# The transpose in a triangular inverse from TensorE in place of a masked merge, beta moved into the decay, and a new plan

## The chip, the cores and the metric

One core of a Trainium2 chip runs the whole program. The metric is device time in microseconds (us) of one execution. An engine is one of five units with an instruction queue of its own that runs in order: TensorE (PE; PEld is its weight load), VectorE (DVE), ScalarE (ACT), GpSimd (POOL) and SyncE (SP, which issues loads).

## The reference, cut to what matters

A two-layer encoder on 256 tokens of width 1024, in float32. Each layer projects the tokens with a wide matrix, runs three mixers side by side (differential attention, a gated delta rule in both directions, windowed attention), merges them through gates, and ends in a gated MLP; each half closes with a layer norm. The change lies in the delta rule, which solves one unit triangular system per head, chunk and direction:

```python
decay = jnp.exp(jnp.where(incl, gc[..., :, None] - gc[..., None, :], -jnp.inf))
kk = jnp.einsum('bhncd,bhnsd->bhncs', kb, k) * decay      # kb = k * beta
a_mat = jnp.where(strict, kk, 0.0) + jnp.eye(C, dtype=kk.dtype)
sol = lax.linalg.triangular_solve(a_mat, rhs, left_side=True, lower=True, unit_diagonal=True)
```

## The kernel before, in words

The weights come in blocks of 512 KB. Each is split on chip into two fp32r parts: ScalarE (or VectorE) copies the block to `hi`, VectorE subtracts to `lo`, and TensorE runs three matmuls for each product (`mm3`). A block thus costs one 128x1024 pass on either engine and, in a channel-major projection, 24 matmuls. There are four `hi`/`lo` pairs (WBUFS) and four landing tiles (RBUFS).

Nothing is issued in the order of the text. Every call on an engine is recorded by `Plan.record` with a cost from `_cost`; `Plan.emit` gives each a rank (the longest chain of costs and of `LATENCY` to the end, plus a priority from `PRIO` by label), and `Plan.schedule` lays the calls out in time, engine by engine. The calls are then issued in the order of these start times, so each engine's queue is fixed beforehand. `A.copy`, `A.scale` and `A.affine` (class `Either`) may go to ScalarE or VectorE, as the plan finds better. The order of the weight blocks is written out (`ORDER`), and their loads keep it (`stream`). All recorded calls carry the line 194 in the profile, so tiles tell them apart.

The delta rule is `gdn`. `decay` makes, for each direction d and half tt of the tokens, exp of the decay differences for four heads (dt_, tag D; 128x512) and a strictly triangular copy (ds_, tag N) by two `affine_select` on GpSimd. Later, `gdn` multiplies k times k (pk, in PSUM), minus beta and ds_ into the matrix N, one head at a time. `solve` then inverts eight 128x128 matrices of one direction at once, by doubling: levels of block size 1, 2, 4, ... 64. It holds the inverse so far (xx) and its transpose (y), both f16. For each level from the second on it makes pv = nt16 x (half of xx), copies it to v16, then makes pp = v16 x (half of y) and px = y x (half of v16); pp is merged into y and px into xx, through a mask with `copy_predicated` for blocks under 32 and by plain copies of sub-blocks above. The two directions run interleaved. pv, pp and px are 8 matmuls each, of 128x64, and each group fills one PSUM bank of the kind "ch", of which there are two (`BANKS`). In the rows, `ch_solve<-a,b` names the moving operand first: `h_solve` is nt16, xx or y, `v_solve` is v16, `id` the identity.

Of the kernel before, what the change touches and what calls it, by code (L numbers as in the profile page):

```python
# [75 lines left out]
def _cost(eng, name, outs, ins, args, kw):  # L76
# [28 lines left out]
    return 0.069 + n / 960 / fast + 0.061 * sum(_columns(ap) == 1 for ap in ins)  # L105
# [32 lines left out]
class Plan:  # L138
# [43 lines left out]
    def record(self, *ways):  # L182
# [36 lines left out]
        op.load = (0.108 if ins[0].dtype in (F32, F32R) else 0.055) if eng == "PE" else 0.0  # L219
# [1283 lines left out]
```

## Time and profile before

| | |
|---|---|
| runs of the kernel | 1000.6 us median of 3 (999.37 to 1002.41) |
| profiled execution | 1000.26 us, of which the span from first to last instruction is 998.6 |
| TensorE clock granted | 0.996 of full speed |
| busy: TensorE / weight load / VectorE / ScalarE / GpSimd | 972.1 / 909.3 / 741.0 / 568.5 / 72.4 us |

How to read it: busy time is the time in which at least one instruction of the engine runs. Idle time of an engine is put down to what released the next instruction. The rows that matter stand two sections below. The stretches with a name in them are: 30 to 50 and 520 to 545 us (`decay` of layer 0 and 1), 70 to 120 and 560 to 612 us (the two solves), 350 to 400 us (a plain stretch of the MLP's projections).

### The profile page before, as it was taken

What the parts mean: (1) busy time and instruction counts of PE and PEld (TensorE: products, weight loads), DVE (VectorE), ACT (ScalarE), POOL (GpSimd) and SP (SyncE); (2) the same over time, 40 slices, a digit from 0 to 9 for tenths busy, and PEclk for the clock granted to TensorE, in tenths of its full rate; (3) what the DMA queues carried; (4) which work ended last, traced back from release to release, by engine and by line L of the source; (5) the groups of instructions that cost most, each with busy time, mean ns of one, the idle gap of its engine ahead of it and who ended that gap; (6) DMA issues with size and microseconds to landing.
All of it is one profiled execution on the core that took longest, in us unless ns stands there. A gap on an engine that the chain in (4) does not pass through costs nothing.

```text
span 998.6 us, 19140 instructions
## 1 busy us (share of the span) xinstructions
PE 972.1 (97%) x7598; PEld 909.3 (91%) x7598; DVE 741.0 (74%) x1362; ACT 568.5 (57%) x1012; POOL 72.4 (7%) x84
## 2 busy tenths in 40 slices
PE   7999999999999999999999989999999999999996
PEld 6898899998988999998889979999999889999885
DVE  7799985675589766675688997866646995677655
ACT  5666865665455654544545876566744655455441
POOL 0510010100000100000006100000000110000000
PEclk9999999999999999999999999999999999999998
DMA  7553344454575655565625423343545855555651
GB/s 269 181 170 100 117 122 151 149 166 140 188 242 167 212 195 188 172 190 188 213 85 190 143 87 119 130 130 111 168 149 174 284 180 164 189 190 177 204 190 43
DMA packets 50109, 165.43 MB, mean 166 GB/s; under 512 B 5751, under 2 KB 11271, under 8 KB 50020
## 3 DMA queue, kind: packets, MB, share of 16 engines
q1 hardware_dynamic: 48644, 159.78, 49.5%
q0 software_dynamic: 1376, 4.43, 1.5%
q8 instruction: 59, 0.97, 0.4%
q14 instruction: 30, 0.25, 0.1%
HBM read 163.12 MB, written 1.07 MB: 164 GB/s over the span
## 4 chain that ended last, share of the span: by engine, by line
PE 79%; DVE 9%; ACT 6%; DMA 3%; issue 2%; POOL 1%; POOLq 0%; ACTq 0%; DVEq 0%
PE mm_proj_ch L194 47%; PE mm_run L194 7%; PE ch_run L194 7%; PE mm_product L194 5%; PE mm_token_major L194 4%; PE at_window L194 2%; DVE lo_take L194 2%; DVE h_solve L194 2%; ACT hi_take L194 1%; DMA G_load_G<-band 1%; PE at_attention L194 1%; DVE z_conv_silu L194 1%; DMA raw_take<-in_w_dram 1%; PE ch_gdn L194 1%; PE ch_solve L194 1%
## 5 line engine op out<-in xcount | busy, mean ns | idle before, releaser
L194 PE MATMUL mm_proj_ch<-xTh,hi_take 128*128 128x256 f32 x1488 | 420.4, 285 | 0.2 <-ACT hi_take L194 0.2
L194 PE MATMUL mm_proj_ch<-xTl,hi_take 128*128 128x256 f32 x1488 | 418.6, 284 | 0.1
L194 PE MATMUL mm_proj_ch<-xTh,lo_take 128*128 128x256 f32 x1488 | 416.3, 284 | 0.5 <-DVE lo_take L194 0.5
L194 ACT ACTIVATE hi_take<-raw_take 128x1024 fp32r<-128x1024 f32 x213 | 223.2, 1057 | 236.4 <-PE mm_proj_ch L194 172.5
L194 DVE TENSOR_TENSOR lo_take<-raw_take,hi_take 128x1024 fp32r<-128x1024 f32 x219 | 267.5, 1232 | 87.7 <-ACT hi_take L194 83.7
L194 PEld LDWEIGHTS mm_proj_ch<-xTh,hi_take 128*128 128x128 f32 x1488 | 279.9, 189 | 3.2 <-issue 1.5
L194 PEld LDWEIGHTS mm_proj_ch<-xTl,hi_take 128*128 128x128 f32 x1488 | 279.8, 189 | 2.3 <-issue 1.2
L194 PEld LDWEIGHTS mm_proj_ch<-xTh,lo_take 128*128 128x128 f32 x1488 | 277.9, 189 | 2.8 <-issue 1.2
L194 ACT ACTIVATE hi_proj_tok<-raw_proj_tok 128x1024 fp32r<-128x1024 f32 x50 | 52.9, 1060 | 66.9 <-PE mm_run L194 36.8
L194 DVE TENSOR_TENSOR lo_proj_tok<-raw_proj_tok,hi_proj_tok 128x1024 fp32r<-128x1024 f32 x50 | 61.0, 1224 | 40.2 <-ACT hi_proj_tok L194 40.0
L194 DVE SCALAR_TENSOR_TENSOR z_conv_silu<-mm_proj_ch,col_params,z_conv_silu 128x254 f32<-128x254 f32 (+1 forms) x96 | 39.4, 474 | 0.9 <-ACT z_conv_silu L194 0.9
L194 ACT ACTIVATE e_window<-e_window,s_window 128x256 f32<-128x256 f32 x59 | 27.8, 500 | 9.4 <-DVE s_window L194 9.4
L194 POOL TENSOR_TENSOR s_tail<-s_tail,nhalf 128x1 f32<-128x1 f32 x8 | 5.7, 712 | 375.5 <-DVE s_tail L194 375.5
L194 ACT ACTIVATE e_attention<-e_attention,s_attention 128x256 f32<-128x256 f32 x48 | 23.0, 500 | 8.6 <-DVE s_attention L194 8.5
L194 PE MATMUL mm_run<-hi_proj_tok,ile_encoder_trunk 128*128 128x512 f32 x88 | 27.4, 390 | 0.0
L194 PE MATMUL mm_run<-hi_proj_tok,tile_encoder_trunk 128*128 128x512 f32 x88 | 27.3, 390 | 0.0
L194 DVE SCALAR_TENSOR_TENSOR g_product<-g_product,mm_product 128x512 f32<-128x512 f32 x24 | 16.5, 686 | 14.1 <-PE mm_product L194 13.8
L194 PEld LDWEIGHTS <-h_solve 128*128 128x128 f16 x448 | 20.4, 98 | 6.9 <-issue 4.0
L194 PE MATMUL mm_product<-ya_attention,hi_take 128*128 128x256 f32 x128 | 25.3, 287 | 0.0
L194 PE MATMUL mm_product<-ya_gdn,hi_take 128*128 128x256 f32 x128 | 23.4, 282 | 0.0
L194 PE MATMUL mm_product<-yc_window,hi_take 128*128 128x256 f32 x128 | 23.4, 283 | 0.0
L194 PE MATMUL ch_run<-hi_proj_tok,ile_encoder_trunk 128*128 128x512 f32 x72 | 22.5, 389 | 0.0
(352 smaller groups left out, 1647.6 us busy)
## 6 DMA issues: line engine op xcount, KB each, us to landing
raw_take<-in_w_dram SPq DMA_DIRECT2D x226, 512.0 KB, 3.8
raw_proj_tok<-in_w_dram SPq DMA_DIRECT2D x60, 512.0 KB, 4.1
G_load_G<-band SPq DMA_DIRECT2D x24, 192.0 KB, 3.4
ya_ln_params<-in_lnp_dram POOLq DMA_DIRECT2D x16, 256.0 KB, 6.3
x<-in_xT_dram SPq DMA_DIRECT2D x4, 256.0 KB, 4.3
x<-in_x_dram SPq DMA_DIRECT2D x2, 512.0 KB, 4.9
out_dram<-x SPq DMA_DIRECT2D x8, 128.0 KB, 1.8
_tile_encoder_trunk<-in_w_dram SPq DMA_DIRECT2D x4, 128.0 KB, 4.3
```

The lines of the kernel that those rows point to most:

```text
L194: op.ways.append((eng, lambda fn=fn, args=args, kw=kw: fn(*args, **kw), _cost(eng, name, outs, ins, args, kw), table))
```

## The change

Three things. (1) In `solve`, the product pp no longer computes the half of y from v16: after px is merged into xx, TensorE multiplies xx with half of the identity, which gives that half of the transpose, and one copy of 128x512 (`A.copy`, on ScalarE or VectorE) puts it into y at every level. (2) `decay` multiplies the strict decay ds_ by minus beta, a column per head, with four ScalarE activations of 128x128; `gdn` then needs one VectorE multiplication of 128x512 in place of four small ones. (3) The plan: other latencies and costs in the planner's model, and other priorities (97 entries for 100, 72 labels in both, none with the same value as before; the solve's own go from 1.6 to 0 in layer 0 and from -1.2 to -7.1 in layer 1). `ORDER` stays as it is.

```diff
-PRIO = {...}
+PRIO = {...}
...
-LATENCY = {"PE": {"PE": 0.0, "ACT": 0.27, "DVE": 0.2, "POOL": 0.2, "SP": 0.2},
-           "ACT": {"PE": 0.27, "ACT": 0.14, "DVE": 0.14, "POOL": 0.18, "SP": 1.42},
-           "DVE": {"PE": 0.26, "ACT": 0.2, "DVE": 0.13, "POOL": 0.18, "SP": 1.22},
+LATENCY = {"PE": {"PE": 0.0, "ACT": 0.22, "DVE": 0.2, "POOL": 0.2, "SP": 0.2},
+           "ACT": {"PE": 0.2, "ACT": 0.14, "DVE": 0.14, "POOL": 0.18, "SP": 1.42},
+           "DVE": {"PE": 0.2, "ACT": 0.2, "DVE": 0.13, "POOL": 0.18, "SP": 1.22},
...
         if outs[0].offset // outs[0].ap[0][0]:
-            return 0.0223
+            return 0.37
...
-    return 0.069 + n / 960 / fast + 0.061 * sum(_columns(ap) == 1 for ap in ins)
+    half = 0.1 if outs[0].ap[0][1] <= 64 and n > 256 else 0.0
+    return 0.069 + half + n / 960 / fast + 0.061 * sum(_columns(ap) == 1 for ap in ins)
...
-        op.load = (0.108 if ins[0].dtype in (F32, F32R) else 0.055) if eng == "PE" else 0.0
+        op.load = (0.108 if ins[0].dtype in (F32, F32R) else 0.029) if eng == "PE" else 0.0
...
         G.affine_select(ds_, dt_, pattern=[[0, NH], [sg, P]], compare_op=ALU.is_gt, fill=0.0, base=0, channel_multiplier=-sg)
+        for h in range(NH):
+            S.activation(ds_[:, h], ds_[:, h], AF.Copy, scale=sc["nbeta"][:, tt, 4 * d + h:4 * d + h + 1])
         return dt_, ds_
...
             xa, yb, va = halves(xx, n)[:, :, :, d], halves(y, n)[:, :, :, 1 - d], halves(v16, n)[:, :, :, d]
+            ib = id16.rearrange("p (k two s) -> p k two s", two=2, s=LEVELS[n])[:, :, 1 - d]
             for h in range(n8):
                 TE.matmul(pv[:, h], nt16[:, h], xa[:, h], start=True, stop=True)
             A.copy(va, pv)
             yield
             for h in range(n8):
-                TE.matmul(pp[:, h], v16[:, h], yb[:, h], start=True, stop=True)
-            for h in range(n8):
                 TE.matmul(px[:, h], y[:, h], va[:, h], start=True, stop=True)
             merge(xx, px, n, 1 - d)
-            merge(y, pp, n, d)
+            yield
+            for h in range(n8):
+                TE.matmul(pp[:, h], xx[:, h], ib, start=True, stop=True)
+            A.copy(yb, pp)
...
             for d in range(2):
                 nt = dec[d, tt][1]
-                for h in range(NH):
-                    nb = sc["nbeta"][:, tt, 4 * d + h:4 * d + h + 1]
-                    V.scalar_tensor_tensor(nt[:, h], pk[:, h], nb, nt[:, h], ALU.mult, ALU.mult)
+                V.tensor_tensor(nt, pk, nt, op=ALU.mult)
                 yf[d, tt] = nt
```

## Rows read from the trace of the kernel before

**Rows 1.** The page's first part: busy time of each engine, share of the span and instructions.

```profile
span 998.6 us, 19140 instructions
PE 972.1 (97%) x7598; PEld 909.3 (91%) x7598; DVE 741.0 (74%) x1362; ACT 568.5 (57%) x1012; POOL 72.4 (7%) x84
```

**Rows 2.** The first matmul in the timeline (start, us, then what it is, with the idle time before it and its releaser), and, from the chain that ended last in order of time, its last piece (start, us, what).

```profile
5.53 0.58 PE L194 MATMUL mm_proj_ch<-xTh,_tile_encoder_trunk 128*128 128x256 f32 x1 [5.53 <-ACT _tile_encoder_trunk L194]
...
959.44 29.93 PE ch_run L194 x132
```

**Rows 3.** Busy time of each engine in stretches: the two solves, a plain stretch, and the two stretches with the decay.

```profile
core 0: us, PE busy (x) PEld busy (x) DVE busy (x) ACT busy (x) POOL busy (x), PEclk, DMA share, GB/s
70.00:120.00 50.00, 46.25 (x570) 43.18 (x568) 47.58 (x108) 36.71 (x71) 2.42 (x5) 1.00 0.37 117
...
560.00:612.00 52.00, 47.83 (x584) 44.22 (x584) 50.32 (x122) 44.65 (x104) 3.40 (x4) 1.00 0.29 93
...
350.00:400.00 50.00, 50.00 (x423) 50.00 (x422) 33.53 (x46) 26.10 (x34) 0.00 (x0) 1.00 0.56 188
...
30.00:50.00 20.00, 19.74 (x135) 16.95 (x134) 14.35 (x18) 12.12 (x19) 11.15 (x11) 1.00 0.49 153
520.00:545.00 25.00, 24.47 (x190) 23.13 (x189) 21.56 (x28) 15.03 (x21) 16.30 (x12) 1.00 0.57 186
```

**Rows 4.** Whom TensorE waited for: us in total, times, longest; the first four in 70 to 120 us, the others in 560 to 612 us.

```profile
engine line waited for: us in total, times, longest us
PE ch_solve L194 <- DVE h_solve L194: 1.7, 5, 0.7
PE ch_solve L194 <- ACT v_solve L194: 0.9, 2, 0.7
PE ch_solve L194 <- ACT h_solve L194: 0.6, 3, 0.2
PE at_attention L194 <- DVE s_attention L194: 0.3, 1, 0.3
...
PE ch_solve L194 <- DVE h_solve L194: 1.2, 2, 0.6
PE ch_solve L194 <- ACT h_solve L194: 0.7, 2, 0.4
PE at_attention L194 <- ACT aT_attention L194: 0.5, 1, 0.5
PE ch_solve L194 <- DVE s_attention L194: 0.5, 1, 0.5
PE mm_proj_ch L194 <- DVE lo_take L194: 0.5, 1, 0.5
```

**Rows 5.** The timeline of one level of layer 0's solve (start, us, what): TensorE's groups of the solve, then VectorE's merges, then ScalarE's copies.

```profile
87.04 0.41 PE L194 MATMUL ch_solve<-v_solve,h_solve 128*128 128x64 f16 x8
87.51 0.40 PE L194 MATMUL ch_solve<-v_solve,h_solve 128*128 128x64 f16 x8
...
88.95 0.40 PE L194 MATMUL ch_solve<-h_solve,v_solve 128*128 128x64 f16 x8 [0.25 <-DVE h_solve L194]
...
90.78 0.39 PE L194 MATMUL ch_solve<-h_solve,h_solve 128*128 128x64 f16 x8
91.39 0.39 PE L194 MATMUL ch_solve<-h_solve,h_solve 128*128 128x64 f16 x8 [0.21 <-DVE h_solve L194]
...
92.18 0.41 PE L194 MATMUL ch_solve<-v_solve,h_solve 128*128 128x64 f16 x8
...
88.18 1.33 DVE L194 CAST_PREDICATED h_solve<-masks,ch_solve 128x512 f16<-128x512 uint8 x2
...
90.00 1.33 DVE L194 CAST_PREDICATED h_solve<-masks,ch_solve 128x512 f16<-128x512 uint8 x2
...
91.22 1.20 ACT L194 ACTIVATE v_solve<-ch_solve 128x512 f16<-128x512 f32 x2 [0.47 <-PE ch_solve L194]
```

**Rows 6.** Groups of instructions of one shape over the whole program: count, busy us, mean ns of one, idle time before them.

```profile
L194 PE MATMUL ch_solve<-h_solve,v_solve 128*128 128x64 f16 x192 | 9.5, 192 | 2.8 <-DVE h_solve L194 1.6 <-DVE s_attention L194 0.5 <-ACT h_solve L194 0.4
...
L194 ACT ACTIVATE h_solve<-ch_solve 32x256 f16<-32x256 f32 x15 | 5.6, 372 | 0.2
...
L194 ACT ACTIVATE h_solve<-ch_solve 64x512 f16<-64x512 f32 x8 | 4.6, 589 | 1.8 <-PE ch_solve L194 1.7
...
L194 ACT ACTIVATE v_solve<-ch_solve 128x512 f16<-128x512 f32 x24 | 14.1, 593 | 8.3 <-PE ch_solve L194 8.1
...
L194 DVE TENSOR_TENSOR v_solve<-ch_solve,h_solve 128x512 f16<-128x512 f32 x8 | 5.4, 683 | 0.0
...
L194 DVE SCALAR_TENSOR_TENSOR N_decay<-ch_gdn,nbeta_gdn_scalars,N_decay 128x128 f32<-128x128 f32 x32 | 8.8, 344 | 0.1
...
L194 DVE TENSOR_TENSOR D_decay<-ch_gdn,D_decay 128x512 f32<-128x512 f32 x8 | 5.1, 685 | 1.2 <-PE ch_gdn L194 1.2
...
L194 ACT ACTIVATE z_finish<-x_scan 128x128 f32<-128x128 f32 x16 | 4.7, 298 | 3.3 <-DVE x_scan L194 3.3
...
L194 ACT ACTIVATE x_scan<-ch_scan,ex_gdn_scalars 128x128 f32<-128x128 f32 x16 | 4.6, 391 | 0.0
...
L194 ACT ACT_TABLE_LOAD x10 | 12.8, 1283 | 1.8 <-PEq L1492 0.8 <-DVE tile_encoder_trunk L194 0.4 <-DVE ile_encoder_trunk L194 0.4
```

**Rows 7.** The same view of VectorE in 70 to 120 us alone.

```profile
L194 DVE CAST_PREDICATED h_solve<-masks,ch_solve 128x512 f16<-128x512 uint8 x16 | 10.7, 700 | 0.0
```

**Rows 8.** The timeline around the decay (start, us, what): GpSimd's last selects of layer 0 and of layer 1, the first use of their result on VectorE in layer 0 and 1, and ScalarE's conversions in layer 1 at that time.

```profile
40.69 2.79 POOL L194 TENSOR_SCALAR_AFFINE_SELECT N_decay<-D_decay 128x512 f32<-128x512 f32 x3
...
538.84 2.39 POOL L194 TENSOR_SCALAR_AFFINE_SELECT N_decay<-D_decay 128x512 f32<-128x512 f32 x4
...
70.67 2.16 DVE L194 SCALAR_TENSOR_TENSOR N_decay<-ch_gdn,nbeta_gdn_scalars,N_decay 128x128 f32<-128x128 f32 x8
...
558.79 1.38 DVE L194 SCALAR_TENSOR_TENSOR N_decay<-ch_gdn,nbeta_gdn_scalars,N_decay 128x128 f32<-128x128 f32 x5
...
535.24 1.06 ACT L194 ACTIVATE hi_take<-raw_take 128x1024 fp32r<-128x1024 f32 x1
540.15 1.06 ACT L194 ACTIVATE hi_take<-raw_take 128x1024 fp32r<-128x1024 f32 x1 [3.86 <-PE mm_proj_ch L194]
```

**Rows 9.** Whom TensorE waited for over the whole program, the row of the solve's merges.

```profile
PE ch_solve L194 <- DVE h_solve L194: 2.8, 7, 0.7
```

More of the change, by code (lines that the diff above doesn't have):

```diff
@@ new lines @@
+PRIO = {(0, 'a', 'ak', 0): -2.6, (0, 'a', 'aq', 1): 1.1, (0, 'a', 0): -0.1, (0, 'a', 1): 8.0, (0, 'a', 2): 6.9, (0, 'a', 3): -2.3, (0, 'ab', 0): -2.2, (0, 'aq', 0): -9.3, (0, 'aq', 1): -4.4, (0, 'c', 'ckv', 0): -20.4, (0, 'c', 'cq', 0): 5.9, (0, 'c', 0): -2.6, (0, 'c', 1): 2.1, (0, 'c', 2): -0.9, (0, 'cq', 0): 5.9, (0, 'cq', 1): 2.3, (0, 'finish'): -6.6, (0, 'gate', 1): 5.2, (0, 'gz', 0): -19.3, (0, 'gz', 1): -1.5, (0, 'gz', 3): -2.8, (0, 'k', 'ab', 0): -1.0, (0, 'k', 'gate', 0): -7.9, (0, 'k', 'gate', 1): 6.1, (0, 'k', 'q', 1): 2.4, (0, 'k', 'v', 0): -2.7, (0, 'k', 'v', 1): 7.3, (0, 'k', 0): -0.9, (0, 'k', 1): -10.1, (0, 'q', 0): 4.4, (0, 'q', 1): 8.0, (0, 'scan'): -3.1, (0, 'v', 0): -0.6, (0, 'v', 1): 4.5, (0, 'wb', 0): 5.9, (0, 'wb', 1): 4.2, (0, 'wb', 2): 4.8, (0, 'wb', 3): -13.0, (0, 'wb', 4): 7.1, (0, 'wb', 5): 4.3, (0, 'wb', 6): 7.1, (0, 'wb', 7): -4.2, (0, 'wb', 8): 0.1, (1, 'a', 'ak', 1): -4.1, (1, 'a', 'aq', 0): -0.2, (1, 'a', 'aq', 1): -4.3, (1, 'a', 0): 0.3, (1, 'a', 1): 3.1, (1, 'a', 3): -0.4, (1, 'ab', 0): -2.2, (1, 'ak', 0): 0.5, (1, 'ak', 1): 1.5, (1, 'aq', 1): 5.7, (1, 'av', 0): 5.4, (1, 'c', 'ckv', 0): 3.0, (1, 'c', 'cq', 0): -2.2, (1, 'c', 0): -3.8, (1, 'c', 1): 1.2, (1, 'ckv', 0): 3.0, (1, 'cq', 0): -1.5, (1, 'finish'): -4.0, (1, 'gate', 0): 7.5, (1, 'gate', 1): -5.5, (1, 'gz', 0): 3.8, (1, 'gz', 10): 4.4, (1, 'gz', 11): -5.4, (1, 'gz', 3): 8.2, (1, 'gz', 4): -3.2, (1, 'gz', 5): 0.4, (1, 'gz', 7): -3.0, (1, 'gz', 8): 14.3, (1, 'gz', 9): -2.7, (1, 'k', 'ab', 0): -3.5, (1, 'k', 'gate', 1): 1.4, (1, 'k', 'k', 0): -0.9, (1, 'k', 'q', 0): 3.4, (1, 'k', 'q', 1): 7.0, (1, 'k', 'v', 0): 3.3, (1, 'k', 'v', 1): 6.9, (1, 'k', 0): 5.2, (1, 'q', 0): 11.6, (1, 'q', 1): 1.6, (1, 'scan'): 0.7, (1, 'solve'): -7.1, (1, 'v', 0): 1.5, (1, 'v', 1): -1.0, (1, 'wb', 0): 8.7, (1, 'wb', 10): 2.6, (1, 'wb', 11): -3.3, (1, 'wb', 2): -2.3, (1, 'wb', 3): 3.1, (1, 'wb', 4): 4.9, (1, 'wb', 5): -1.6, (1, 'wb', 6): 2.9, (1, 'wb', 7): 9.9, (1, 'wb', 8): 3.9, (1, 'wb', 9): -0.1}
```

1 line of the change is left out of this document (removed).

## The prediction

> **What bounds the kernel now.** I read the page first: TensorE (PE) is busy in 972.1 of 998.6 us and VectorE in 741.0 [rows 1]. Two parts of PE's 26.5 us of idle time lie outside this change: 5.5 us before the first matmul and 9.2 us after the last one (998.6 less the end of the last run of matmuls, 959.44 + 29.93) [rows 2]. That leaves 11.8 us. Then the busy time by stretch: in 70 to 120 us and 560 to 612 us, where the two layers solve their triangular systems, PE is busy 46.25 of 50 and 47.83 of 52 us, and in a plain projection stretch 50.00 of 50 [rows 3]. So 3.75 + 4.17 = 7.92 us of the 11.8 are lost in the solves. The reader should see in the same rows what is full there: VectorE, 47.58 of 50 and 50.32 of 52, and in layer 1 nearly ScalarE too, 44.65 of 52. Third, who made PE wait: results of the solve's merges and other VectorE work [rows 4].
>
> One level of the solve shows how [rows 5]. The operand named first is the moving one, so (v, h) is px, (h, v) is pp and (h, h) is pv. px of both directions runs at 87.04 and 87.51; two masked merges follow at 88.18; only then pp, at 88.95, with a PE wait put down to VectorE although pp's operands (v16, yb) were there long before. What it waited for must be room in PSUM: there are two "ch" banks and two directions, and a merge is what empties a bank. The next two merges start at 90.00, pv follows at 90.78 and 91.39 (again a wait on VectorE), the copies to v16 at 91.22, px again at 92.18. A level is thus three bank holds in a row, about 5.1 us for both directions, of which VectorE's merges are two. Filling matmuls run between, but PE takes instructions in its given order and stops at the solve's when a merge is late.
>
> **The change, part by part.**
>
> The second merge. Per level and direction, 8 matmuls pp = v16 x yb become 8 matmuls of xx against half the identity: same count, same 128x64 f16 shape, 24 groups of 8, so PE's cost is nil (192 matmuls, 9.5 us, stay 192) [rows 6]. Four of six levels lose a masked merge: 16 of the 32 in the program, 8 a layer. Sixteen of them keep VectorE 10.7 us in layer 0's stretch, 0.67 each [rows 7], so 5.35 us a layer go. The two upper levels lose their plain copies of y, 2 + 1 a direction: 4 x 0.372 + 2 x 0.589 = 2.7 us a layer, mostly ScalarE's [rows 6]. Added are 12 copies a layer of 128x512 from PSUM to f16, on ScalarE or VectorE as the planner likes: ScalarE's copy of the same shape into v16 takes 0.593, so 7.1 us a layer [rows 6]. On VectorE the nearest row is the 128x512 subtraction into v16 at 0.683, 8.2 us. I take ScalarE: its copies in the solve are there now.
>
> The decay. 16 small multiplications a layer on VectorE (32 in 8.8 us, so 0.275 each, 4.4 us) become 4 of 128x512 (the like of them, D_decay, takes 0.685: 2.74 us): 1.66 us a layer less, right ahead of the solve, where VectorE is its chain [rows 6]. Added are 16 ScalarE operations a layer of 128x128 with a pointer for scale, SBUF to SBUF, not in this trace. Nearest rows: 0.298 (z_finish, SBUF to SBUF) and 0.391 (x_scan, pointer scale from PSUM; its 16 fill 4.6 us, so 0.29 each in a row) [rows 6]. That is 4.6 to 6.3 us a layer; I take 4.6, as they run in a row. What hides it: N_decay leaves GpSimd at 541.23 in layer 1 and is first used at 558.79 (43.48 and 70.67 in layer 0), a slack of 17 and 27 us [rows 8]. Its wait is new: ScalarE now stands for GpSimd's last select, and behind it are queued the next hi conversions. At 536 to 540 ScalarE stood idle for 3.86 us because PE had not freed a weight buffer [rows 8]; four buffers were full. I price it at 0; if the buffers were empty there it would cost up to the 4.9 us from 536.30 (the end of ScalarE's conversion) to 541.23, once, plus 0.3 to 0.4 for each scaling.
>
> The Trainium skill speaks against this part ("ScalarE: Activation LUTs", Rules for kernel authors: multiplications belong on VectorE, not ScalarE). In the rows above the two engines take 0.29 and 0.275 for the same 128x128, so the trace puts the choice on which engine is full.
>
> Loads by stretch: VectorE loses 5.35 + 1.66 = 7.0 us: 47.58 becomes 40.6 of 50, and 50.32 becomes 43.3 of 52. ScalarE gains 7.1 - 2.7 = 4.4: 36.71 becomes 41.1, and 44.65 becomes 49.1 of 52 (94%). The scalings lie before the solve, in stretches with ScalarE at 12.12 of 20 and 15.03 of 25 [rows 3].
>
> The plan. Priorities and model costs alone change; the order of weight blocks (ORDER) and SyncE's load order (stream) stay, so I price queues of loads at 0. A new order may add or drop ScalarE table loads, 1.28 us each, ten now [rows 6]; I take none. What it does to PE outside the solves has no row; the bounds are the 3.9 us of idle that are left there (11.8 - 7.9), as a gain, and as much again as a loss.
>
> **The sum.** Of PE's named waits in the two solves I let go those whose cause is relieved: for merges on VectorE 1.7 + 1.2, for other late VectorE work 0.3 + 0.5 + 0.5, for ScalarE's h_solve copies, half of which are y's, 0.6 + 0.7. That is 2.6 + 2.9 = 5.5 us [rows 4]. The waits for v_solve (0.9) and aT (0.5) stay. Below, the bound is 0. Above, it is all the time in which PE loads no weights in the solves, 50 - 43.18 and 52 - 44.22: 14.6 us [rows 3]. I stay near the lower row, as part of the 14.6 is the switch between f32 and f16 matmuls, whose groups remain as many. Profiled execution: 1000.26 (span 998.6 and 1.7 around it) less 5.5 is 994.8. The median of the runs lies 0.3 higher, 1000.6, so the forecast is 995.1.
>
> The Trainium skill ("Perfetto Trace Analysis", Identifying the Most-Contended Engine) holds matmul busy time for a bad measure and weight-load time for a good one. By that the head room in the solves is the 14.6 us, and all of it would give 986.
>
> **The rivals.**
>
> (a) The gain goes on to ScalarE or into the new plan. In layer 1 ScalarE would stand at 94%, and PE's waits turn from "VectorE h_solve" into "ScalarE h_solve" or "v_solve". Layer 1's 2.9 us stay: 1000.6 - 2.6 = 998.0. An order that loses 2 to 4 us elsewhere comes out at 997 to 1000. For: the copies all come from one full engine to another, and the two engines' work in a stretch falls by 2.6 us only. Against: the planner may put a copy on either, and layer 0 has room on both.
>
> (b) Slower: y now hangs behind xx. Before, pp needed only v16 and the old y and could run while xx was being merged; now pp can't start until the merge of xx has ended, and px of the next level waits for pp's copy. If pv and pp do not run side by side (two banks, two directions), 24 groups each get a wait. PE's seven present waits on VectorE's h_solve total 2.8 us, 0.40 each [rows 9]: 24 x 0.40 = 9.6, less 5.5, gives 1000.6 + 4.1 = 1004.7. It decides from the point where y's copy ends later than that of v16. Against: in rows 5 pp already comes after the merges of xx, for want of a bank.
>
> (c) More: the freed VectorE, a solve that begins 1.66 us sooner and a plan that fills the gaps take most of the 14.6 us and some of the 3.9: about 986.
>
> (d) The change does not do what it says: the planner puts y's copies on VectorE (0.683 for 0.67 saved). Then VectorE is relieved by 1.66 us alone and the time stays within 2 us of 1000.6; I count it with (a).
>
> **How the numbers follow.** A difference of 0.3% (3.0 us) is about what can be told from no change here. Forecast (990 to 997.6, taken at 995.1): 0.50. (a) with (d), 997.6 to 1003.6: 0.24. (b): 0.14. (c), 982 to 990: 0.12. Faster is the forecast and (c), 0.62; same 0.24; slower 0.14. The range leaves out the tails of (b) and (c): 986, all of the weight-load gap, to 1004, just short of (b)'s price.
>
> **What would show it.** In the changed profile: 16 CAST_PREDICATED for 32; a new group of matmuls with the identity as the moving operand, 192; VectorE near 41 and 43 us in the two solve stretches, ScalarE up by about 4; PE's busy time there nearer the full stretch, and its waits on VectorE h_solve below 1 us. Eight N_decay multiplications of 128x512 and 32 ScalarE scalings at 0.29 to 0.39, none of which is followed by a PE wait for hi_take. The forecast is wrong if VectorE's load falls as said and PE's idle time in the solves doesn't: then the three bank holds, not VectorE, set the pace; or if it falls and idle time turns up between 125 and 290 or 625 and 800 us, where the plan alone has changed things.

## The result, and the profile after

The changed kernel takes 994.14 us (median of 6 runs, 992.73 to 995.61) against 1001.23 (6 runs, 999.37 to 1003.17). The ratio is 0.9928, 95% interval 0.9912 to 0.9943: 7.1 us less, where 5.5 less was forecast. In the profiled executions the span goes from 998.6 to 991.0 us, 7.6 us. In all that follows, the lines of the recording helper are L195 where before had L194 (L196 and others in the experiments); nothing else hangs on them.

The page's first part, after (it answers to [rows 1]):

```profile
span 991.0 us, 19154 instructions
PE 969.0 (98%) x7598; PEld 906.2 (91%) x7598; DVE 722.3 (73%) x1310; ACT 588.8 (59%) x1068; POOL 73.0 (7%) x84
```

The reader should see three numbers. TensorE runs as many matmuls as before, and its idle time falls from 26.5 us to 991.0 - 969.0 = 22.0. Its busy time falls as well, by 3.1 us. The recorded lengths of the matmuls, added up, do not fall (2207 us before, 2211 after), so the matmuls did not become faster; they stand closer together, and holes shorter than a matmul lie hidden in busy time. VectorE loses 18.7 us, ScalarE gains 20.3: the engines' work was exchanged, not reduced.

Busy time by stretch, after (stretch, its length, PE, PEld, DVE, ACT, POOL with counts, clock, DMA share, GB/s): the two stretches of [rows 3], then, within them or beyond, the six levels of layer 0's solve and of layer 1's (from the first px to the last copy), and one stretch of layer 0's later part, which stands last as it was before:

```profile
70.00:120.00 50.00, 49.50 (x612) 47.16 (x611) 43.45 (x86) 44.63 (x88) 2.27 (x4) 1.00 0.38 116
560.00:612.00 52.00, 51.83 (x607) 50.20 (x608) 42.59 (x93) 42.46 (x86) 4.76 (x4) 1.00 0.39 114
78.90:119.20 40.30, 39.80 (x526) 37.80 (x524) 33.75 (x68) 37.09 (x76) 0.00 (x0) 1.00 0.34 105
568.80:631.70 62.90, 62.90 (x729) 61.32 (x728) 51.86 (x115) 50.27 (x100) 2.25 (x3) 1.00 0.42 130
425.00:450.00 25.00, 23.36 (x138) 20.37 (x137) 16.32 (x21) 11.08 (x14) 0.00 (x0) 1.00 0.55 169
...
425.00:450.00 25.00, 25.00 (x164) 22.96 (x164) 17.90 (x23) 11.75 (x14) 0.00 (x0) 1.00 0.62 191
```

TensorE's idle time in the two solve stretches was 7.92 us and is 0.50 + 0.17 = 0.67: 7.25 us come from here. Time without a weight load was 14.6 us there and is 2.84 + 1.80 = 4.6. The same stretches now hold 612 and 607 matmuls, where they held 570 and 584. VectorE is no longer full, and ScalarE stands as high as VectorE. The last two rows are the other side: TensorE was busy for all 25.00 us of that stretch before, and for 23.36 now. Taken as a ledger of idle time: 5.5 us at the start and 9.2 at the end are as before, 0.67 is left in the solves, so 22.0 - 15.4 = 6.6 us lie elsewhere, where there were 3.9.

Whom TensorE waited for, after: in 70 to 120 us, in 560 to 612 us, and (the last two) rows of the whole program (us in total, times, longest). They answer to [rows 4, 9]:

```profile
PE ch_solve L195 <- ACT h_solve L195: 0.2, 1, 0.2
...
PE ch_gdn L195 <- DVE kk_gdn L195: 0.5, 1, 0.5
...
PE mm_run L195 <- ACT tile_encoder_trunk L195: 1.2, 1, 1.2
PE mm_token_major L195 <- DVE xTl L195: 0.9, 2, 0.5
```

The first two are all named waits in the two stretches: not one on a masked merge is left there, and the waits for v_solve, aT and s_attention are gone too. The 1.2 us before mm_run lie in the 425 to 450 us stretch; before has no such row.

Groups by shape over the whole program, after (they answer to [rows 6, 7]):

```profile
L195 ACT ACTIVATE v_solve<-ch_solve 128x512 f16<-128x512 f32 x24 | 14.1, 599 | 0.6 <-PE ch_solve L195 0.6
L195 ACT ACTIVATE h_solve<-ch_solve 128x512 f16<-128x512 f32 x24 | 13.8, 588 | 0.1
L195 DVE CAST_PREDICATED h_solve<-masks,ch_solve 128x512 f16<-128x512 uint8 x16 | 11.1, 712 | 3.1 <-PE ch_solve L195 3.0
...
L195 ACT ACTIVATE N_decay<-N_decay,nbeta_gdn_scalars 128x128 f32<-128x128 f32 x32 | 9.9, 388 | 3.5 <-POOL N_decay L195 3.4
L195 PE MATMUL ch_solve<-id,h_solve 128*128 128x64 f16 x192 | 9.7, 194 | 0.3 <-ACT h_solve L195 0.2
...
L195 DVE TENSOR_TENSOR N_decay<-ch_gdn,N_decay 128x512 f32<-128x512 f32 x8 | 5.2, 681 | 0.4 <-PE ch_gdn L195 0.4
```

Sixteen masked merges for 32, all 24 copies of y on ScalarE at 588 ns, 192 matmuls with the identity as moving operand at the price of the old ones. A masked merge takes 712 ns (703 before), and VectorE now waits 3.1 us in all for the products that it merges, where it waited 0.1 before: it comes before the result, where it came after it.

One level of layer 0's solve, after, as in [rows 5] (start, us, what): TensorE, then VectorE, then ScalarE:

```profile
85.68 0.41 PE L195 MATMUL ch_solve<-v_solve,h_solve 128*128 128x64 f16 x8
...
87.45 0.41 PE L195 MATMUL ch_solve<-id,h_solve 128*128 128x64 f16 x8
...
89.19 0.39 PE L195 MATMUL ch_solve<-h_solve,h_solve 128*128 128x64 f16 x8
...
90.91 0.40 PE L195 MATMUL ch_solve<-v_solve,h_solve 128*128 128x64 f16 x8
...
86.40 1.37 DVE L195 CAST_PREDICATED h_solve<-masks,ch_solve 128x512 f16<-128x512 uint8 x2
...
88.56 1.06 ACT L195 ACTIVATE h_solve<-ch_solve 128x512 f16<-128x512 f32 x2
...
90.27 0.60 ACT L195 ACTIVATE v_solve<-ch_solve 128x512 f16<-128x512 f32 x1
```

The level did not get shorter. Three bank holds still follow one another: px (the second direction's at 85.68, the first's at 85.23), merge at 86.40, the turned xx at 87.45, y's copy at 88.56, pv at 89.19, v's copy at 90.27, px again at 90.91. That is 5.7 us from px to px, where [rows 5] have 5.1. What changed is that no matmul here has a wait put down to it: each eviction ends before TensorE, filled with other matmuls, comes to what needs the bank.

The end of the chain that ended last, after (start, us, what), which answers to [rows 2]: 951.89 + 29.93 = 981.82, 9.2 us before the end as before.

```profile
951.89 29.93 PE ch_run L195 x132
```

ScalarE's timeline around layer 1's decay, after, and TensorE's one wait there, which answer to [rows 8]:

```profile
536.46 2.75 ACT L195 ACTIVATE N_decay<-N_decay,nbeta_gdn_scalars 128x128 f32<-128x128 f32 x9 [3.41 <-POOL N_decay L195]
539.12 2.94 ACT L195 ACTIVATE hi_take<-raw_take 128x1024 fp32r<-128x1024 f32 x3
...
540.21 0.38 PE L195 MATMUL mm_proj_ch<-xTh,hi_take 128*128 128x256 f32 x1 [0.49 <-ACT hi_take L195]
```

The conversion that TensorE waits for at 540.21 is the first of the three that were queued behind the scalings.

### The profile page after: what moved, and what is told of

The parts are those of the page before. It is cut to its first block, busy times and chain, and to the rows that moved or that the text cites. A ratio compares the mean times of both kernels' runs of the same rounds, so it can differ in the third digit from the quotient of the medians.

```text
span 991.0 us, 19154 instructions
## 1 busy us (share of the span) xinstructions
PE 969.0 (98%) x7598; PEld 906.2 (91%) x7598; DVE 722.3 (73%) x1310; ACT 588.8 (59%) x1068; POOL 73.0 (7%) x84
## 4 chain that ended last, share of the span: by engine, by line
PE 81%; DVE 6%; ACT 4%; DMA 2%; POOL 1%; issue 1%; POOLq 0%; DVEq 0%; ACTq 0%
PE mm_proj_ch L195 48%; PE ch_run L195 6%; PE mm_product L195 6%; PE mm_run L195 6%; PE mm_token_major L195 3%; PE at_window L195 2%; PE at_attention L195 2%; PE ch_solve L195 2%; DMA raw_proj_tok<-in_w_dram 2%; PE ch_gdn L195 1%; ACT hi_take L195 1%; PE ch_scan L195 1%; DMA raw_take<-in_w_dram 1%; PE ch_finish L195 1%; POOL x_decay L195 1%
## 5 line engine op out<-in xcount | busy, mean ns | idle before, releaser
L195 PE MATMUL mm_proj_ch<-xTh,hi_take 128*128 128x256 f32 x1488 | 421.8, 286 | 0.9 <-ACT hi_take L195 0.5
L195 PE MATMUL mm_proj_ch<-xTl,hi_take 128*128 128x256 f32 x1488 | 420.2, 285 | 0.0
L195 PE MATMUL mm_proj_ch<-xTh,lo_take 128*128 128x256 f32 x1488 | 419.1, 285 | 0.0
L195 DVE TENSOR_TENSOR lo_take<-raw_take,hi_take 128x1024 fp32r<-128x1024 f32 x219 | 266.8, 1232 | 104.5 <-ACT hi_take L195 86.4
L195 ACT ACTIVATE hi_take<-raw_take 128x1024 fp32r<-128x1024 f32 x214 | 224.4, 1057 | 195.0 <-PE mm_proj_ch L195 136.5
L195 PEld LDWEIGHTS mm_proj_ch<-xTh,hi_take 128*128 128x128 f32 x1488 | 280.2, 189 | 3.5 <-ACT hi_take L195 1.8
L195 PEld LDWEIGHTS mm_proj_ch<-xTh,lo_take 128*128 128x128 f32 x1488 | 279.5, 189 | 2.8 <-issue 1.6
L195 PEld LDWEIGHTS mm_proj_ch<-xTl,hi_take 128*128 128x128 f32 x1488 | 280.2, 189 | 1.6 <-issue 0.8
L195 ACT ACTIVATE hi_proj_tok<-raw_proj_tok 128x1024 fp32r<-128x1024 f32 x50 | 52.8, 1060 | 66.8 <-PE mm_run L195 37.9
L195 DVE TENSOR_TENSOR lo_proj_tok<-raw_proj_tok,hi_proj_tok 128x1024 fp32r<-128x1024 f32 x50 | 61.0, 1223 | 42.9 <-ACT hi_proj_tok L195 42.9
L195 DVE SCALAR_TENSOR_TENSOR z_conv_silu<-mm_proj_ch,col_params,z_conv_silu 128x254 f32<-128x254 f32 (+1 forms) x96 | 39.1, 474 | 0.6 <-ACT z_conv_silu L195 0.5
L195 DVE SCALAR_TENSOR_TENSOR g_product<-g_product,mm_product 128x512 f32<-128x512 f32 x24 | 16.5, 686 | 24.5 <-PE mm_product L195 24.5
L195 POOL TENSOR_TENSOR s_tail<-s_tail,nhalf 128x1 f32<-128x1 f32 x8 | 5.3, 665 | 380.4 <-DVE s_tail L195 380.4
L195 ACT ACTIVATE e_window<-e_window,s_window 128x256 f32<-128x256 f32 x55 | 26.5, 498 | 10.5 <-DVE s_window L195 10.4
L195 PEld LDWEIGHTS <-h_solve 128*128 128x128 f16 x640 | 25.8, 98 | 4.2 <-ACT h_solve L195 0.4
L195 PE MATMUL mm_run<-hi_proj_tok,tile_encoder_trunk 128*128 128x512 f32 x88 | 27.5, 392 | 1.6 <-ACT tile_encoder_trunk L195 1.2
L195 PE MATMUL mm_run<-hi_proj_tok,ile_encoder_trunk 128*128 128x512 f32 x88 | 27.3, 391 | 0.0
L195 ACT ACTIVATE e_attention<-e_attention,s_attention 128x256 f32<-128x256 f32 x46 | 22.7, 503 | 5.3 <-DVE s_attention L195 5.1
L195 PE MATMUL mm_product<-ya_attention,hi_take 128*128 128x256 f32 x128 | 25.1, 287 | 0.0
L195 PE MATMUL mm_product<-ya_gdn,hi_take 128*128 128x256 f32 x128 | 23.7, 283 | 0.0
L195 PE MATMUL mm_product<-yc_window,hi_take 128*128 128x256 f32 x128 | 23.7, 283 | 0.0
L195 ACT ACTIVATE tile_encoder_trunk<-tile_encoder_trunk 128x512 f32<-128x512 f32 (+1 forms) x22 | 13.6, 625 | 16.6 <-DVE tile_encoder_trunk L195 16.6
```

The lines of the kernel that those rows point to most:

```text
L195: op.ways.append((eng, lambda fn=fn, args=args, kw=kw: fn(*args, **kw), _cost(eng, name, outs, ins, args, kw), table))
```

## The experiments

The theory to start with was the prediction's: VectorE was full in the solves, and the two edits relieve it. The rivals: the searched plan did it; the place of the merges in the chain of a level matters, not VectorE's load; and, for what was lost elsewhere, the planner's new latencies. Ratios are to the kernel before on the same chip (medians 1001.0 to 1001.5).

**Edits and plan apart.** ops_old_plan has the new operations with the old priorities and model costs; plan_only the old operations with the new ones.

```diff
-PRIO = {(0, 'a', 'ak', 0): -2.6, ...
+PRIO = {(0, 'a', 'ak', 0): 2.8, ...
-LATENCY = {"PE": {"PE": 0.0, "ACT": 0.22, ...
+LATENCY = {"PE": {"PE": 0.0, "ACT": 0.27, ...
```

(ops_old_plan against the changed kernel; plan_only is the reverse against the kernel before.)

> Both edits of the operations (transpose by TensorE with a copy, beta in the decay) under the old priorities and the old model costs. My theory, that the operations themselves free VectorE in the two solves: the solves' share of the gain comes back without a new plan, 4 to 8 us under the kernel before (993 to 997). Rival, that the new plan is what brings it: within 2 us of the kernel before, or slower, as an order searched for other operations is now out of place.

> The operations of the kernel before under the new priorities and model costs. My theory: no gain in the solves, the loss of some 4 us in the MLP stretches stays, so 1000 to 1006. Rival, the plan: 4 to 7 us faster than the kernel before.

Measured: ops_old_plan 1005.46 us, 1.0050 (1.0038 to 1.0062); plan_only 1003.36, 1.0029 (1.0018 to 1.0040). Each half alone is slower than before, and the two together are 7.1 us faster. The starting theory, that the operations bring the gain in any order, falls here. The windows of ops_old_plan show how; the third row is the six levels of layer 1:

```profile
70.00:120.00 50.00, 48.11 (x598) 45.16 (x597) 38.28 (x60) 38.57 (x65) 3.60 (x4) 1.00 0.40 119
560.00:612.00 52.00, 47.92 (x596) 44.05 (x594) 44.45 (x106) 44.92 (x104) 4.46 (x6) 1.00 0.30 88
...
570.20:600.60 30.40, 27.85 (x406) 24.51 (x405) 23.05 (x53) 29.41 (x72) 1.36 (x2) 1.00 0.25 72
```

VectorE's load falls further than forecast in layer 0 and nearly as far in layer 1 (38.28 and 44.45 us, forecast 40.6 and 43.3), and TensorE still idles 1.89 + 4.08 = 5.97 us. Over the whole program it waits in the solves for other things:

```profile
PE ch_solve L194 <- ACT h_solve L194: 2.1, 5, 0.7
PE ch_solve L194 <- DVE v_solve L194: 1.8, 2, 1.6
```

Layer 1's levels take 30.4 us here, with 406 matmuls in them; VectorE is busy for 23.05 us and ScalarE for 29.41, all but full. This comes near rival (a): under the old priorities the solve is hurried, the freed VectorE goes unused, and TensorE waits for copies on ScalarE (2.1 us) and, at the end of layer 1's solve, for VectorE's v_solve (1.8). Outside the two stretches TensorE idles for 1005.3 - 975.6 (its busy time by the page) - 5.97 = 23.7 us, where before had 26.5 - 7.92 = 18.6: the rest of the loss, 5 us, lies there, spread over many stretches. In plan_only layer 0's solve was profiled at a granted clock of 0.90, so that window is not read further. Layer 1's levels ran at 1.00:

```profile
585.50:650.00 64.50, 63.75 (x723) 61.76 (x722) 55.99 (x127) 47.73 (x103) 2.30 (x3) 1.00 0.42 131
```

With the old operations, masked merges included, TensorE idles for 0.75 us there. In layer 1 the new plan, which starts this solve later and draws it out, thus takes the idle time away by itself; what it loses lies elsewhere.

**No search at all.** The same pair with an empty table of priorities and the new model costs, so that neither side has an order searched for it.

```diff
-PRIO = {(0, 'a', 'ak', 0): -2.6, ...
+PRIO = {}
```

> The operations of the kernel before, the new model costs, and no priorities at all (an order that nobody searched). It is the lower half of a pair on equal footing. Theory, that the operations free VectorE in the solves under any order: this one is slower than its twin with the new operations by 4 to 9 us. Rival, that what was gained is only a search fitted to the new operations: the two lie within 2 us. I expect about 1012 here.

> The new operations, the new model costs, no priorities: the other half of the pair. Theory: 4 to 9 us faster than the twin with the old operations, the difference in the two mixer stretches; rival: within 2 us of it. I expect about 1006.

Measured: none_before 1016.29 us, 1.0142 (1.0125 to 1.0159); none_after 1018.43, 1.0169 (1.0154 to 1.0185). With the new operations nothing is gained here, and 2.1 us are lost. The windows of none_before over its own levels say why:

```profile
78.00:115.00 37.00, 36.69 (x507) 34.92 (x506) 36.29 (x60) 27.26 (x45) 0.00 (x0) 1.00 0.44 137
578.00:622.00 44.00, 43.45 (x556) 41.60 (x556) 41.23 (x74) 33.25 (x60) 0.61 (x2) 1.00 0.44 139
```

VectorE is as full as in [rows 3] (36.29 of 37 and 41.23 of 44 us), and TensorE idles for 0.31 + 0.55 us only: there is nothing for the new operations to give back. A full VectorE beside the solve does not by itself cost TensorE anything. The waits lie elsewhere, but for one of 2.6 us in the solve; none_after, whole program:

```profile
PE at_window L195 <- ACT aT_window L195: 4.8, 5, 1.6
PE at_window L195 <- DVE s_window L195: 3.4, 5, 1.6
PE mm_run L195 <- DVE z_product L195: 3.3, 2, 1.6
PE mm_run L195 <- ACT z_product L195: 3.2, 2, 1.6
PE ch_solve L195 <- DVE h_solve L195: 2.6, 1, 2.6
```

So whole-plan comparisons can't say what an edit is worth: each draws a new order, and orders differ by more than the edit. The rest holds the order fixed.

**The same order, one edit undone.** An operation gets a second call, `swap`, used only when instructions are emitted. The planner sees the changed kernel, and each engine's program is laid out from the changed kernel's plan, except for the swapped operation. In the traces of all six kernels made this way TensorE's 7598 matmuls follow one another by tiles as in the changed kernel, so the same matmul can be found in two traces and its delay read.

```diff
-            op.call()
+            (op.swap or op.call)()
```

merge_back puts the 16 masked merges of y on VectorE again (TensorE still turns xx over); copy_on_dve puts all 24 copies of y on VectorE as plain copies; decay_back leaves the 32 scalings out and multiplies by beta in the old 32 small operations.

```diff
# merge_back
+            plan.ops[-1].swap = lambda yb=yb, m=m, pp=pp: nc.vector.copy_predicated(yb, m, pp)
...
# copy_on_dve
+            plan.ops[-1].swap = lambda yb=yb, pp=pp: nc.vector.tensor_copy(yb, pp)
...
# decay_back
+            plan.ops[-1].swap = lambda: None
...
+                        nc.vector.scalar_tensor_tensor(nt[:, h], pk[:, h], nb, nt[:, h], ALU.mult, ALU.mult)
```

> The changed kernel with its order of instructions on every engine held fixed; only at emission the copy of y at the four masked levels is swapped for a masked merge on VectorE, 16 in all. The transposes by TensorE stay. My theory (which engine carries it decides): VectorE takes back 16 x 0.7 us in the solves, TensorE waits for VectorE's h_solve again, and 3 to 7 us of the gain go: 997 to 1001. Rival (the shorter chain by the order px, merge, transpose decides, not the engine): within 1.5 us of the changed kernel.

> The changed kernel with its order held fixed; at emission the 32 ScalarE scalings of the decay are left out and each VectorE multiplication of 128x512 becomes the four of 128x128 with beta. My theory: VectorE's extra 0.4 us an operation lies ahead of the solve, not in it, so under 1.5 us slower than the changed kernel (994 to 996). Rival, that the decay carries a good part: 2 to 4 us slower.

> The changed kernel with its order held fixed; at emission all 24 copies of y go to VectorE as plain copies. If the engine decides, VectorE takes 24 x 0.68 us, more than with the 16 masked merges put back (which came out at 999.2): 999 to 1003. Rival, that the masked merge is slow as an instruction or that its mask costs: clearly faster than that, 994 to 997.

Measured: merge_back 999.23 us, 0.9981 (0.9972 to 0.9990), 5.1 above the changed kernel; decay_back 995.37, 0.9941 (0.9929 to 0.9953), 1.2 above, which its interval doesn't tell from 0; copy_on_dve 1001.55, 1.0001 (0.9988 to 1.0013), 7.4 above. A plain copy takes VectorE 682 ns there and a masked merge 706 in merge_back, so the mask itself adds little. The windows of merge_back and its longest wait in the solves, then the windows of copy_on_dve, then layer 1's of decay_back:

```profile
70.00:120.00 50.00, 47.54 (x576) 44.53 (x575) 44.93 (x87) 37.32 (x71) 4.17 (x5) 1.00 0.37 117
560.00:612.00 52.00, 49.62 (x574) 46.73 (x573) 47.63 (x99) 37.25 (x71) 6.95 (x6) 1.00 0.35 109
...
PE ch_solve L196 <- DVE h_solve L1046: 1.6, 5, 0.5
```

```profile
70.00:120.00 50.00, 47.18 (x574) 44.25 (x573) 45.43 (x87) 36.40 (x70) 4.32 (x5) 1.00 0.39 117
560.00:612.00 52.00, 49.67 (x575) 46.72 (x574) 48.25 (x100) 36.72 (x74) 6.94 (x6) 1.00 0.35 112
```

```profile
560.00:612.00 52.00, 49.68 (x588) 47.68 (x587) 44.90 (x106) 42.59 (x86) 3.29 (x4) 1.00 0.35 105
```

TensorE idles 2.46 + 2.38 us again in merge_back, with 0.67 in the changed kernel, and its waits are mostly for merges of h_solve (1.6 us for those put back, 0.8 for those of xx; 0.8 for v_solve). In decay_back the 1.2 us by the medians are not told from 0, but the trace shows where the edit works: TensorE idles for 2.32 us in layer 1's stretch, where the changed kernel has 0.17, as layer 1's solve begins 1.9 us later against the work before it, and the wait for hi_take at 540 us is gone.

One reservation holds for merge_back and copy_on_dve and for the next two kernels. In their profiled executions TensorE has done 162 matmuls between 5 and 35 us, ahead of the first solve, where the changed kernel has done 171 (164 in act_ballast). That is some 2 us that the edit doesn't explain. If it stands in all their executions, the merges are worth about 3 us and not 5.1. The profiled pair points the other way: merge_back's matmuls are 2.0 us late as layer 0's solve begins and 5.4 as it ends, 4.8 as layer 1's begins and 8.4 as it ends, so 7.1 us arise in the solves (9.0 in copy_on_dve). But this pair lies 8.4 us apart and the medians 5.1, as merge_back's profiled execution lies 1.9 us above its median and the changed kernel's 1.4 below. That the cost arises in the solves is not in doubt; its size is known only as 3 to 7 us.

**Load or place.** If an engine's load is what costs, idle work of the same length beside the chain of the solve must cost as much as the masked merges. If the place in the chain is what costs, such work is nearly free. dve_ballast and act_ballast add, right behind each of 16 copies of y, one operation that writes a scratch tile that nobody reads, on VectorE and on ScalarE.

```diff
+                    op.call()
+                    nc.vector.tensor_tensor(scratch, bc_mid(ident, 4), bc_mid(UI, 4), op=ALU.mult)   # dve_ballast
+                    nc.scalar.activation(scratch, bc_mid(ident, 4), AF.Copy)                          # act_ballast
```

> The changed kernel with its order held fixed; behind each of the 16 copies of y at the four masked levels VectorE gets an idle task of 128x512 (a product of two constants into a scratch tile that nobody reads, about 0.69 us). The copies stay on ScalarE. Theory A, VectorE's load decides: as with the masked merges put back (about the same load), 998 to 1001. Theory B, it is the merge's place in the chain (it waits in VectorE's queue and holds its PSUM bank until done): the idle task delays only what is queued behind it, so less than half of that loss, 994.5 to 997.

> The same idle task on ScalarE instead, 16 copies of 128x512 into the scratch tile, about 0.62 us each, order held fixed. In the changed kernel's solve of layer 0 ScalarE is the fuller engine (37.1 of 40.3 us, VectorE 33.8). If the fuller engine sets TensorE's waits, this costs more than the idle task on VectorE: 997 to 1001. If room on ScalarE is left, as my forecast had it for layer 0, within 2 us of the changed kernel.

Measured: dve_ballast 1000.18 us, 0.9995 (0.9983 to 1.0008), 6.0 above the changed kernel; act_ballast 999.82, 0.9981 (0.9972 to 0.9991), 5.7 above. What was added, in the one and in the other, and the windows of each:

```profile
L1047 DVE TENSOR_TENSOR scratch<-tri 128x512 f16<-128x512 f32 x16 | 11.0, 685 | 0.1
...
70.00:120.00 50.00, 47.41 (x578) 44.48 (x577) 45.04 (x87) 41.33 (x80) 4.34 (x5) 1.00 0.38 117
560.00:612.00 52.00, 49.38 (x576) 46.66 (x575) 48.06 (x100) 40.67 (x83) 6.95 (x6) 1.00 0.35 111
```

```profile
L1047 ACT ACTIVATE scratch<-tri 128x512 f16<-128x512 f32 x16 | 10.0, 627 | 0.0
...
70.00:120.00 50.00, 47.32 (x576) 44.68 (x576) 40.40 (x80) 44.57 (x88) 3.80 (x5) 1.00 0.38 117
560.00:612.00 52.00, 49.62 (x577) 47.05 (x577) 43.33 (x93) 44.43 (x94) 7.20 (x7) 1.00 0.38 118
```

Work that nobody waits for costs what the merges cost, on either engine, and the waits take the name of the loaded engine: over the whole program 1.9 us on VectorE's h_solve in the one, 3.1 us on ScalarE's v_solve in the other. The theory of the place falls, in the form in which it was put, with less than half of the loss. Ten to eleven us of work cost 5.7 to 6.0 us (3.7 to 4.0 without the 2 us at the start; 6.7 by the delays within the solves of the profiled executions). ScalarE is thus as tight as VectorE in the new order; the higher cost that was expected of the fuller engine did not come. Each idle task stands in its engine's queue ahead of the chain's next merge or copy, in an order that was laid out without it. These runs therefore don't tell load as such from a late place in the queue; a task put elsewhere in the stretch was not tried.

**The other direction.** no_y_copy takes 16 copies of y off ScalarE in the same order (y then misses the entries that they would write).

```diff
+            if LEVELS[n] < 32:
+                plan.ops[-1].swap = lambda: None
```

> The changed kernel with its order held fixed and the 16 copies of y at the four masked levels left out (y then misses its entries of these levels; everything else runs). It is the ballast with its sign turned. If time in the solves goes on following the work of the two engines as with ballast (5 to 6 us for 10 to 11 us of work), taking away 16 x 0.59 = 9.4 us gives 4 to 5 us more: 989 to 990. If the changed kernel's solves are bound by TensorE by now (0.67 us of idle time left in the two stretches), under 1.5 us: 992.5 to 994.

Measured: 994.03 us, 0.9930 (0.9908 to 0.9951), the changed kernel's time. Its windows:

```profile
70.00:120.00 50.00, 49.65 (x615) 47.29 (x614) 43.75 (x86) 41.19 (x80) 2.51 (x5) 1.00 0.37 117
560.00:612.00 52.00, 51.45 (x604) 49.59 (x603) 43.31 (x94) 39.36 (x77) 4.76 (x4) 1.00 0.35 111
```

ScalarE stands 3.4 and 3.1 us lower, TensorE the same (0.90 us idle), and neither solve is more than 0.4 us shorter. The changed kernel stands at a knee: some 10 us more on either engine cost about half their length, and 16 copies fewer bring nothing, because TensorE is full.

**What was lost elsewhere.** Idle time outside the solves grew from 3.9 to 6.6 us. old_latency_mlp gives the old latencies to the operations that carry no label of a mixer, the later part of a layer among them; solve_prio_back puts the old priorities of the solve into the new table, to see whether its stretching in layer 1 (levels over 62.9 us) matters.

```diff
-        return op.lat if op.lat is not None else LATENCY[op.eng][n.eng]
+        return op.lat if op.lat is not None else (LATENCY if op.label else LATENCY0)[op.eng][n.eng]
...
```

> The changed kernel, with the old latencies in the planner's model for all operations without a label (layer norms and MLP), the new ones for the mixers. Theory, that the changed kernel's 5.0 us of loss in the stretches that the operations don't touch comes from the lower latencies, by which an instruction is queued before its data are there: 2 to 5 us faster than the changed kernel, 989 to 992, if the mixers keep their order. Rival, that the loss is an accident of the order: within 2 us, either way.

> The changed kernel with two numbers of its plan put back: the priority of the solve, 1.6 for 0 in layer 0 and -1.2 for -7.1 in layer 1. In the changed kernel layer 1's levels take 62.9 us (40.9 before) and TensorE loses next to nothing in them. Theory, that a late and stretched solve in layer 1 is the new plan's part of the gain: the levels of layer 1 come back to about 40 us and 2 to 5 us are lost: 996 to 999. Rival, that the stretch is without effect: within 1.5 us.

Measured: old_latency_mlp 993.38 us, 0.9916 (0.9900 to 0.9933); solve_prio_back 995.21, 0.9945 (0.9926 to 0.9963). Neither can be told from the changed kernel. The row that was to vanish in old_latency_mlp is still there:

```profile
PE mm_run L199 <- ACT tile_encoder_trunk L199: 1.2, 1, 1.2
```

So the latencies are not seen to be the cause. Whether the stretched solve earns anything was tested only in part: from the first to the last write from PSUM into xx or y, layer 1's levels took 43.9 us before and 65.1 after, and in solve_prio_back still 53.4. Taking back that half of the stretching costs nothing that can be seen. Why the later part of layer 0 loses what it loses stays open. The row of 1.2 us is in the runs with the new model costs, searched or not, and not in before or ops_old_plan; which of these costs brings it was not tried. No kernel here clearly beats the changed one.

## Why the prediction was right, and where its sum was off

**What bounds.** The reading of [rows 3, 4] holds as to the place: TensorE's idle time in the two solves falls by 7.25 us, and the span by 7.6. That work put back on VectorE brings such idle time back is shown by merge_back and dve_ballast, in the new order. That VectorE's load as such made it in the old order is not shown: work added on ScalarE does the same (act_ballast), and ops_old_plan and none_before speak against it. The level as three bank holds [rows 5] is right as a description and turned out not to be the limit: the holds are all still there, and TensorE loses nothing. The condition that I named for being wrong, VectorE's load falling and TensorE's idle time staying, nearly came true in ops_old_plan, under the old priorities, with 5.97 of 7.92 us left; and in none_before VectorE is full and TensorE hardly waits. In layer 1 the new plan removes the idle time even with the old operations (plan_only). The forecast therefore needed the new plan more than it said: by the medians the same operations take 1005.46 us under the old plan and 994.14 under the new one, some 11 us apart, where the plan was priced at 0 with bounds of 3.9 us. That the total came out near the forecast is in part luck.

**The second merge.** 16 merges for 32, 192 matmuls at 9.7 us for 9.5, 24 copies at 588 ns where 593 was assumed, all on ScalarE as assumed. VectorE was forecast at 40.6 and 43.3 us and is at 43.45 and 42.59; ScalarE at 41.1 and 49.1, and is at 44.63 and 42.46. The forecasts held the work in the stretch constant. But 42 and 23 more matmuls run there now, which bring their own conversions and evictions, and layer 1's solve runs on past 612 us. In the levels of layer 0 ScalarE has become the fuller engine, 37.09 us of 40.3 against 33.75.

**The decay.** 8 multiplications at 681 ns, as assumed. The 32 scalings take 9.9 us, 0.31 each, where 0.29 was taken from a bound of 0.29 to 0.39; a scaling by itself takes 388 ns, close to the row of x_scan, 391. Their price of 0 was right. The new wait came as described: ScalarE stood 3.41 us for GpSimd's select, within the bound of 4.9. Its price was not quite 0: the first of the three conversions queued behind it starts at 539.12, and TensorE waits 0.49 us for it at 540.21, which the prediction had named as a sign against it. In decay_back, without the scalings, that wait is gone. That the whole edit gains is not shown by the times: undoing it costs 1.2 us, which the runs don't tell from 0.

**The plan.** Priced at 0 with bounds of 3.9 us on either side, it lost 2.7 us of idle time outside the solves. A gain that was forecast at 5.5 and measured at 7.1 is thus made of a larger gain in the solves and a loss that the sum had at nothing. Counted from start to start, TensorE's steps into, within and out of the solve's groups of f16 matmuls took 46.7 us before and 36.7 after, 10.0 less, and all its other steps 2.5 more.

**The sum.** The step that failed in size is "of PE's named waits in the two solves I let go those whose cause is relieved", 5.5 us. Nearly all of the idle time there went, 7.25 of 7.92. The waits that were to stay (v_solve 0.9, aT 0.5) went too, since work on both engines shifted under them. By the time without a weight load 10.0 of 14.6 us came back; that agrees with 7.25 us of idle time and most of the 3.1 us by which TensorE's busy time fell, the holes that busy time hides and that the named waits don't list. The Trainium skill ("Perfetto Trace Analysis", Identifying the Most-Contended Engine) calls weight-load time the better measure of TensorE's head room. In the solves these rows bear that out, as the steps counted above also fell by 10.0 us; over the whole program both measures fell by the same 4.5 us. The whole gap was still too much to forecast, as 4.6 us of it are left with TensorE full. The reason that the prediction gave, the switch between f32 and f16 matmuls, accounts for part: before, 2.2 us of the gap stood where a weight load for f16 follows one for f32, 0.04 us each.

**The rivals.** (a), the gain goes on to ScalarE or into the plan: half true. It is what happened under the old plan (ops_old_plan). Under the new one ScalarE is as tight as VectorE (act_ballast), but TensorE became full first (no_y_copy), and the plan's loss is 2.7 us. (b), y behind xx, 24 waits of 0.40: not seen. y's copy does hang behind xx, but one wait of 0.2 us on ScalarE's h_solve is what is left, because each hold has other matmuls in it. (c), most of the weight-load gap: near it in the solves alone, not in the whole. (d), copies on VectorE: it did not happen, and copy_on_dve shows its price: 1001.55, the time before. The prediction's count for (d) was off, though the time it gave was met: it set one copy at 0.683 us against one merge at 0.67, but a layer has 12 copies, 8.2 us, against 8 merges, 5.35, so VectorE would not have been relieved by 1.66 us but loaded with 1.2 more.

**What carries the gain.** In the new order, undoing the merge edit costs 5.1 us and the decay edit 1.2, together 6.3 of 7.1 (some 4 if the 2 us at the start are taken off); that the two prices add up was not tried. In the old order the same operations cost 4.4 us against the kernel before. My reading is that the operations make room and that only an order which spreads the solve over that room turns it into time. The first half is shown for the new order; the second is argued from ops_old_plan, and solve_prio_back, which takes back half of the spreading, shows no loss.

## What to carry to other kernels

Where a planner orders the instructions, an edit has no price of its own: value it with the order held fixed, by swapping the call when it is emitted, and judge the order and the edit together. Such a price belongs to that order, which was laid out for the changed operations: a plan made anew for the old ones might lose less. Test whether an engine is the limit with a pair, idle work added and work taken away: a cost on one side and nothing on the other says that the kernel stands where two limits meet, and that the next gain is not on that engine. And where an engine is full in a stretch, look at the idle time of the bounding engine there, not only at its named waits; the short holes count too.

## What the runs showed that I had not expected

Idle work costs about the same on VectorE and on ScalarE: 6.0 us for 11.0 us of it, and 5.7 for 10.0. A masked merge of 128x512 from PSUM to f16 takes 0.70 to 0.71 us on VectorE, a plain copy of the same shape 0.68 there (copy_on_dve) and 0.59 on ScalarE. And four kernels that differ from the changed one only inside the solves had done 7 to 9 matmuls fewer by 35 us, in three of them with a wait of 0.5 to 0.6 us for a load of the bias table's one-hot input. So had old_latency_mlp, whose span is the changed kernel's (991.1 us). What makes this was not tried.
